# Block transposes on VectorE in place of TensorE's, in the second mixture of experts of a two-block network

## The chip, the core and the metric

The kernel runs on one core of a Trainium2 chip. The metric is the device time of one execution in microseconds (us). Three runs of the kernel before gave 2225.45, 2225.75 and 2227.01 us, median 2225.75.

## What is computed

Two blocks over 256 tokens of 1024 features, all in float32. The first block has gated linear attention, dilated attention and a mixture of 32 experts. The second block has two layers of three mixers each, followed by a dense feed-forward layer (layer 0) or a mixture of 8 experts (layer 1), a gated embedding and at the end a norm. The change touches the mixture of 8 experts:

```python
def moe_swiglu(x, router_w, router_b, w1, w3, w2):
    logits = (x @ router_w + router_b).astype(jnp.float32)
    top_v, top_i = lax.top_k(logits, TOP_K)
    top_p = jax.nn.softmax(top_v, axis=-1)
    gate = jnp.sum(jax.nn.one_hot(top_i, N_EXPERTS_2, dtype=jnp.float32) * top_p[..., None], axis=-2)
    out = jnp.zeros_like(x)
    for e in range(N_EXPERTS_2):
        out = out + gate[..., e:e + 1] * swiglu(x, w1[e], w3[e], w2[e])
    return out
```

where `swiglu(x, w1, w3, w2)` is `(silu(x @ w1) * (x @ w3)) @ w2`, with 1024 features, 2816 hidden features and 2 experts a token.

## The kernel before

The phases run one after another: block 1, its mixture (`moe1`), then mixers, feed-forward and embedding of layer 0, mixers of layer 1, the second mixture (`moe2`, phase `ffn1`), the embedding of layer 1 and the last norm. All large weights come through one `Stream` in the order of their use, in tiles of 1 MB, issued from SyncE's queue (L262). The stream has a ring of 3 buffers, which the phase `ffn1` widens by 6, so a tile can be issued when TensorE is done with the tile 9 before it.

`moe2` takes the experts in two halves of four (`c` = 0, 1), with 96 slots for each expert. The 384 slots of a half are three row tiles of 128 (`r`). At first the tokens are gathered into `xg`. Then a half has eleven passes (`j`), each over 256 of the 2816 hidden features. A pass has three parts:

- `first_products` multiplies the gathered tokens by eight tiles of `w1` and `w3` (`k`), 12 matmuls a tile, each on 32 columns of TensorE with 512 columns of weights moving. The sums are in three PSUM banks, slots on partitions: 256 columns for `w1` and 256 for `w3` of every row tile.
- ScalarE takes the SiLU of the first 256 columns into a tile `ft` (L301), and VectorE multiplies by the second 256 (L1981). `ft` has four buffers, and a pass uses three.
- `post` (L1984 to L1989) brings these onto partitions by hidden feature, as the second product needs them. Six 128x128 transposes on TensorE (L231) fill two PSUM banks, one of which ScalarE copies into `hT` and the other VectorE. `post` is kept in the list `later`, and `flush` runs it after two tiles of the following pass (`k == 2`).

After the eleven passes come the down products: two halves of the output features (`d`), each of 22 tiles `w2` against the 22 slices `hT[:, k]`. The last `post` of a half is flushed after two of these tiles. `combine` puts the results back to the tokens and adds them to `x`. In pass 5 of the second half stands `overflow`, a loop over the experts that got more than their 96 tokens, run 0 times or once. Its flag is loaded by every engine (L970) and followed by a branch that joins the engines (L971).

The scheduler of the language places each engine's instructions in a queue of its own, by the order of the program and by what it expects of their times; the waits between engines are semaphores that it sets. All eight PSUM banks are one ring, given out in turn by `bank`.

Of the kernel before, what the change touches and what calls it, by code (L numbers as in the profile page):

```python
# [14 lines left out]
PSUM = bass.MemoryType.PSUM  # L15

D, S = 1024, 256
RING = 3
# [3 lines left out]
# buffers of 1 MB that each phase adds to the ring's RING  # L22
WIDE = {"b1": 0, "moe1": 9, "mix0": 0, "mix1": 0, "ffn0": 2, "ffn1": 6, "ple0": 4, "ple1": 4, "fin": 0}
# buffers for the parts of weights; tokens that an expert takes at first
SPLIT = 4
CAP1, CAP2 = 32, 96
# the phases that begin with a router: its weights and their number
ROUTED = {"moe1": ("wr", 36), "ffn1": ("wr2", 8)}
# of the norms before the phases that take x split, with the norm's factors applied to the products
GAIN = {"b1": "n1g", "mix0": "g_mix0", "mix1": "g_mix1", "ffn0": "g_ffn0", "ple0": "g_ple0", "ple1": "g_ple1"}  # L30
# the mixers: buffers of 2 KB a partition, steps beside each step of a dense product (at first and later), attention units at once
V2, RATE, RATE2, LANES = 15, 1, 4, 2
# the mixers' outputs in the order in which their product with w_out takes them
# [5 lines left out]
# ---------------------------------------------------------------- host: layouts and shape constants  # L39
def _consts():  # L40
    f = np.float32
# [7 lines left out]
    # GLA: sums of log decays from the middle of a token's chunk, and from the middle of the chunk before  # L49
# [25 lines left out]
    # RWKV: sums from the middle of the chunk (token 63), inclusive and exclusive  # L75
# [4 lines left out]
    # of the 64 x 64 blocks on the diagonal  # L80
# [33 lines left out]
def _kt(w, kc):  # L114
    """[kc*128, C] -> [128, kc*C]"""
    c = w.shape[1]
    return w.reshape(kc, 128, c).transpose(1, 0, 2).reshape(128, kc * c)


def prep(I):  # L120
# [7 lines left out]
    # vectors, a column per 128 features  # L128
# [22 lines left out]
    # block 1: tiles in the order of their use; attention by heads  # L151
# [13 lines left out]
    # block 2  # L165
# [50 lines left out]
# ---------------------------------------------------------------- the program  # L216
class Bank:
    """One PSUM bank. The first matmul on a quadrant clears the bank's written bits there."""
# [15 lines left out]
class Stream:  # L234
    """The large weights in the order of their use, in tiles of up to 1 MB, through a ring of buffers that a
    phase can widen"""
# [39 lines left out]
class Kern:  # L276
# [6 lines left out]
    # ---- helpers  # L283
# [3 lines left out]
    def act(self, out, in_, func, **kw):  # L287
        """an activation; Ln and Exp from the table set that has both, loaded after the last of another set"""
# [16 lines left out]
    def after(self, ins):  # L305
        """what is traced inside goes behind ins in its engine's queue"""
        if ins is None or ins[0] is not self.nc.cur_bb:
            return ExitStack()
        return self.tc.issue_after(ins[1].ins if hasattr(ins[1], "ins") else ins[1])
# [13 lines left out]
    def rstd(self, src, n, scale, eps, floor=None, out=None):  # L323
        """1 / sqrt(src * scale + eps), src in PSUM, from an estimate and a Newton step"""
# [17 lines left out]
    def changed(self, x, k, n=2, late=False):  # L342
        """chunks k .. k + n - 1 of x are final: their squares for the next norm, and x * gain in two parts.
        late: the squares some steps of the next dense product later"""
# [29 lines left out]
    def add_squares(self):  # L374
# [4 lines left out]
        for i in range(sq.shape[1]):  # L379
# [4 lines left out]
            for t in range(2):  # L384
                ts = slice(128 * t, 128 * t + 128)
                b.mm(b.t[:, t:t + 1], sq[:, i, ts], ones[:, 0:1])
                # and their part of the router's logits
                self.lastsum = b.mm(b.t[:, 2 + n * t:2 + n * t + n], x[:, k + i, ts],
                                    self.sm1[:, o + n * (k + i):o + n * (k + i) + n])

    def sum_squares(self):
        """of x's features: for all partitions a row over the tokens, or, before a router, a column for each 128 of
        them, followed by the logits of x"""
# [9 lines left out]
    def factors(self, pool, more=None):  # L403
        """the norm's factor of each token, as rows and as columns, once the next dense product has begun"""
# [15 lines left out]
    def scaled(self, out, p):  # L420
        """products of the norm's input [128, n, 256], times the factors"""
        self.nc.vector.tensor_tensor(out, p, self.row[:, None, :].to_broadcast([128, p.shape[1], S]), op=ALU.mult)  # L422

    def weights(self, kc, ncol):
        """k, first column, then hi and lo parts of up to 512 columns of the k-th 128 rows of the next weights"""
# [14 lines left out]
    # ---- work that goes on beside the dense products: generators, advanced in turn between their steps  # L440
    def beside(self, gen, late=False):
        """late: the first part waits for its turn too"""
# [27 lines left out]
    def mm3(self, b, n, w, c, h, k):  # L470
        """chunk n of 128 features from a piece of weights that starts at column c, k-th chunk of the input"""
# [6 lines left out]
    def dense_fm(self, h, evict, kc=8, ncol=512, stagger=False):  # L478
        """features of the output on partitions; evict(n, ap) gets pairs of 128-feature chunks. stagger: the second
        half of the products goes pair by pair"""  # L480
# [17 lines left out]
    def dense_tm(self, h, evict, kc=8, ncol=512):  # L498
        """tokens on partitions; evict(t, ap[128, ncol]) per token tile"""
# [22 lines left out]
    # ---- the whole  # L522
# [100 lines left out]
    def prepare(self):  # L623
        """what later phases need of the small inputs"""
# [12 lines left out]
    # ---- block 1: gated linear attention, dilated attention, branch gates  # L637
    def block1(self, x, early):
        """early() makes room for the next phase's weights"""
# [66 lines left out]
    def gla(self, work, raw, h, a2, oraw, graw):  # L706
# [11 lines left out]
        def log_decay():  # L718
            """tokens on partitions"""
# [27 lines left out]
        def before(hd):  # L747
            """decays from and to the middles of the chunks"""
# [16 lines left out]
        def after(hd, kin, qin, qx, eB):  # L765
            hs = slice(hd * 128, hd * 128 + 128)
            # inside the chunks
# [11 lines left out]
            # between them: the state in the frame of the middle of each chunk  # L779
# [123 lines left out]
    # ---- the mixtures of experts  # L903
    def first_max(self, pool, x, n, tag):
        """max over the last axis of x [128, 2, n], and a one-hot of its first place"""
# [13 lines left out]
    def top2(self, pool, el, n):  # L919
        """the two largest of each token: one-hots and values"""  # L920
# [5 lines left out]
    def places(self, pool, oh1, oh2, n, beside):  # L926
        """each token's place in its experts' lists, from 1, and 0 where it is in none"""
# [17 lines left out]
    def shares(self, pool, oh1, oh2, m1, m2, n, group=None):  # L945
        """each token's weights of its two experts, by a softmax of their logits; times group"""
# [16 lines left out]
    def overflow(self, pool, x, xs, rs, wo, fi, n, units, w13, w2):  # L963
        """Experts with more than cap tokens: those past cap go through here, an expert at a time over all
        tokens, with weight 0 for the others. units loops over the fours of experts and, inside, over 256 hidden
        features of one of them at a time."""
# [55 lines left out]
    def route_in(self, work, x, n, b0, htm=None):  # L1022
        """RMS factors and logits with tokens on partitions; hi and lo of the tokens, not normed: the latter's last
        step is left to be done"""
# [26 lines left out]
    def gathered(self, out, htm, P, g):  # L1051
        """a one-hot's slots of tokens times g, feature-major: out's tiles [128, 8, n], each from a first slot, for
        P [128, 2, slots]"""
# [16 lines left out]
    def of_slots(self, out, P, col):  # L1070
        """a column of the tokens, gathered by a one-hot: for each 128 slots a column of out"""
# [7 lines left out]
    def keep_input(self, pool, x, g, rs):  # L1079
        """x * g, for the tokens past an expert's share"""  # L1080
# [5 lines left out]
    def over_flag(self, pool, Wt, ps, n, cap):  # L1086
        """weights of the tokens past their expert's first cap, and 1 if there are any"""
# [12 lines left out]
    def moe1(self, x):  # L1100
        tc, nc = self.tc, self.nc
        ident = self.cst("ident")
        with tc.tile_pool(reuse_waits="tile", name="m1", bufs=1) as pool:
# [4 lines left out]
            # only the chosen group's experts stay  # L1108
# [7 lines left out]
            # one-hots token -> (expert, slot), for 8 experts at first  # L1116
# [9 lines left out]
            def gather(n):  # L1126
                """the tokens of 8 experts"""
# [5 lines left out]
            def rest():  # L1133
# [4 lines left out]
                # a token's chosen group has the largest logit: its share is 1 / the sum of exp(logit - max)  # L1138
# [9 lines left out]
                # their weighted transposes  # L1148
# [88 lines left out]
    # ---- block 2: the three mixers  # L1237
    def rope(self):
        """the angles, to within pi, whose sines are cos and sin of position * frequency: [128 (2 heads x 64), 2, 256]"""
# [26 lines left out]
    def mix(self, l, x):  # L1266
        tc, nc, A = self.tc, self.nc, self.A
        with tc.tile_pool(reuse_waits="tile", name="mix", bufs=1) as pool:
# [17 lines left out]
            f = {}                              # tensors that are ready  # L1286
# [25 lines left out]
    def add_pairs(self, x, banks, late):  # L1312
        """the last products (pieces of weights, first column, input and its chunk) pair by pair, added to x"""
# [19 lines left out]
    def shifted(self, T, h):  # L1333
        """the RWKV columns, mixed with those of the token before"""
# [19 lines left out]
    def rwkv(self, T, z, w0, f, out):  # L1354
        """RWKV-7 in chunks of 128 tokens; heads 2c, 2c+1 are the halves of chunk c of the features"""
# [7 lines left out]
        # log decays (tokens on partitions), a and g  # L1363
# [17 lines left out]
        # normalised keys  # L1381
# [12 lines left out]
        # operands in the frame of the middle of each chunk, tokens (2, 128) last  # L1394
        dec = T("dec", (128, 2, 2, 2))         # feature chunk, token chunk: exp(end - mid), exp(mid - start)
        rT = self.cst("rT")
        tv = lambda ap: ap.rearrange("p (t s) -> p t s", t=2)
        ar, bk = [], []                        # token chunk, alpha | rho and beta | kappa
# [20 lines left out]
        # scores [j, i] of every head and chunk: beta.alpha, beta.rho, kappa.alpha, kappa.rho  # L1419
        sc = T("sc", (128, 8, 4, 128))         # token chunk and head  # L1420
# [13 lines left out]
        # inverse of I + L by doubling blocks up to 64, M and its transpose, for all heads and chunks  # L1434
# [18 lines left out]
        # beside it: tokens on partitions for v of both chunks, beta and kappa of the first; g; the bonus  # L1453
# [32 lines left out]
        # the two chunks in turn  # L1486
        yT = V2t("yT")
        st = T("st", (128, 2, 128))            # the state, heads on the diagonal blocks
        nc.gpsimd.memset(st, 0.0)
        for t in range(2):  # L1490
# [12 lines left out]
            # U0 = M0 R0, U1 = M1 (R1 - L10 U0)  # L1503
# [15 lines left out]
            if not t:  # L1519
                # the state after the first chunk, in the frame of the middle of the second  # L1520
# [12 lines left out]
            # y [v, i]  # L1533
# [525 lines left out]
```

## Time and profile before

| | |
|---|---|
| median of three runs | 2225.75 us |
| span of the profiled execution, first to last instruction | 2222.0 us |
| TensorE busy (matmuls) | 2066.5 us, 93% |
| VectorE busy | 825.3 us, 37% |
| ScalarE busy | 641.0 us, 29% |
| GpSimd busy | 23.7 us, 1% |
| moved by DMA | 613.39 MB, mean 276 GB/s |
| mean granted TensorE clock | 0.979 |

The time of the profiled execution itself is not listed apart from its span; the median of the runs is 3.75 us above the span. Busy shares are means over phases with different limits, so a change in one phase is read from that phase. Tile `w` is a weight tile, `ps` a PSUM bank, `xg`, `rawh` and `rawl` hold gathered tokens, `ft` the gated hidden features, `hT` their transposes. L228 is the matmul of the helper class `Bank` and L231 its transpose, L301 the helper for activations, so groups are told apart by their tiles.

### The profile page before, as it was taken

What the parts mean: (1) busy time and instruction counts of PE and PEld (TensorE: products, weight loads), DVE (VectorE), ACT (ScalarE), POOL (GpSimd) and SP (SyncE); (2) the same over time, 40 slices, a digit from 0 to 9 for tenths busy, and PEclk for the clock granted to TensorE, in tenths of its full rate; (3) what the DMA queues carried; (4) which work ended last, traced back from release to release, by engine and by line L of the source; (5) the groups of instructions that cost most, each with busy time, mean ns of one, the idle gap of its engine ahead of it and who ended that gap; (6) DMA issues with size and microseconds to landing.
All of it is one profiled execution on the core that took longest, in us unless ns stands there. A gap on an engine that the chain in (4) does not pass through costs nothing. (4 is left out here: it accounts for less than half of the span.)

```text
span 2222.0 us, 39268 instructions
## 1 busy us (share of the span) xinstructions
PE 2066.5 (93%) x16772; PEld 1250.0 (56%) x16772; DVE 825.3 (37%) x1736; ACT 641.0 (29%) x1320; POOL 23.7 (1%) x33
## 2 busy tenths in 40 slices
PE   7999998787577779999999999999999999999997
PEld 6999994122222238889999898743333333233236
DVE  5787663000000027777666877510000010000005
ACT  5466642000000025356556635310010000001005
POOL 0000000000000010000000000000000000000000
PEclk9999999999799999999999999899999999999999
DMA  5344577999899983325554331579999999799972
GB/s 175 117 143 152 185 308 298 420 420 419 357 420 419 420 348 114 107 67 205 193 184 171 130 117 58 207 280 382 392 400 383 388 369 384 294 419 393 406 307 93
DMA packets 88632, 613.39 MB, mean 276 GB/s; under 512 B 9879, under 2 KB 12071, under 8 KB 18560
## 3 DMA queue, kind: packets, MB, share of 16 engines
q1 hardware_dynamic: 86272, 604.74, 70.2%
q0 software_dynamic: 1344, 5.10, 0.7%
q8 instruction: 134, 2.20, 0.4%
q10 hardware_dynamic: 832, 0.94, 0.1%
q14 instruction: 50, 0.41, 0.1%
HBM read 609.69 MB, written 1.05 MB: 275 GB/s over the span
## 5 line engine op out<-in xcount | busy, mean ns | idle before, releaser
L228 PE MATMUL ps<-w,xg 128*32 128x512 f32 x2432 | 392.0, 599 | 67.5 <-DMA w<-wgu 43.0
L340 DVE TENSOR_TENSOR wl<-w,wh 128x512 fp32r<-128x512 f32 (+2 forms) x500 | 318.7, 652 | 166.5 <-ACT wh L339 158.0
L339 ACT CAST wh<-w 128x512 fp32r<-128x512 f32 (+2 forms) x500 | 289.7, 585 | 294.8 <-PE ps L228 229.4
L228 PE MATMUL ps<-w,hT 128*32 128x512 f32 x2624 | 338.5, 594 | 30.4 <-DMA w<-wdn 24.9
L228 PEld LDWEIGHTS ps<-w,xg 128*32 128x32 f32 x2432 | 89.2, 110 | 315.1 <-issue 199.0
L228 PE MATMUL ps<-rawh,wh 128*128 128x256 f32 x896 | 258.2, 288 | 0.0
L228 PE MATMUL ps<-rawh,wl 128*128 128x256 f32 x896 | 252.2, 282 | 1.5 <-DVE rawl L353 1.4
L228 PE MATMUL ps<-rawl,wh 128*128 128x256 f32 x896 | 252.1, 282 | 0.0
L228 PEld LDWEIGHTS ps<-w,hT 128*32 128x32 f32 x2624 | 90.4, 110 | 262.7 <-issue 188.5
L228 PE MATMUL ps<-w,rawl 128*32 128x512 f32 x1408 | 175.8, 599 | 5.4 <-issue 5.4
L228 PEld LDWEIGHTS ps<-rawh,wh 128*128 128x128 f32 x896 | 169.9, 190 | 4.2 <-issue 1.4
L228 PEld LDWEIGHTS ps<-rawh,wl 128*128 128x128 f32 x896 | 170.1, 190 | 3.2 <-DVE rawl L353 1.6
L228 PEld LDWEIGHTS ps<-rawl,wh 128*128 128x128 f32 x896 | 170.2, 190 | 1.1 <-DVE ast L1789 0.2
L228 PE MATMUL ps<-w,rawh 128*32 128x512 f32 x1408 | 168.3, 595 | 0.0
L1981 DVE SCALAR_TENSOR_TENSOR ft<-ps,rsl,ft 128x256 f32<-128x256 f32 x66 | 31.9, 484 | 313.6 <-ACT ft L301 313.2
L301 ACT ACTIVATE ft<-ps,rsl 128x256 f32<-128x256 f32 x66 | 31.3, 474 | 343.6 <-PE ps L228 343.6
L228 PE MATMUL ps<-hh,wh 128*128 128x256 f32 x416 | 125.8, 303 | 0.0
L228 PE MATMUL ps<-hh,wl 128*128 128x256 f32 x416 | 117.4, 284 | 0.1
L228 PE MATMUL ps<-hl,wh 128*128 128x256 f32 x416 | 117.2, 282 | 0.0
L228 PEld LDWEIGHTS ps<-w,rawl 128*32 128x32 f32 x1408 | 45.5, 110 | 103.6 <-issue 103.3
L228 PEld LDWEIGHTS ps<-w,rawh 128*32 128x32 f32 x1408 | 43.9, 110 | 97.9 <-issue 97.5
L1204 DVE SCALAR_TENSOR_TENSOR sg<-ps,rsl,sg 128x512 f32<-128x512 f32 x8 | 6.0, 750 | 206.7 <-PE ps L228 173.4
(495 smaller groups left out, 2727.0 us busy)
## 6 DMA issues: line engine op xcount, KB each, us to landing
w<-m SPq DMA_DIRECT2D x264, 1024.0 KB, 7.3
w<-wgu SPq DMA_DIRECT2D x128, 1024.0 KB, 19.9
w<-wdn SPq DMA_DIRECT2D x64, 1024.0 KB, 19.9
w<-f SPq DMA_DIRECT2D x32, 1024.0 KB, 5.2
w<-wz SPq DMA_DIRECT2D x20, 1024.0 KB, 4.9
w<-wdh SPq DMA_DIRECT2D x24, 768.0 KB, 4.3
w<-wb SPq DMA_DIRECT2D x16, 1024.0 KB, 4.9
w<-wo SPq DMA_DIRECT2D x8, 1024.0 KB, 5.3
```

Of the source, the lines that this page charges most:

```text
L228: return self.k.nc.tensor.matmul(out, lhsT, rhs, start=new, stop=stop, skip_group_check=True, **kw)
L301: r = sc.activation(out, in_, func, **kw)
L339: self.nc.scalar.copy(h, src)
L340: self.nc.vector.tensor_sub(l, src, h.bitcast(F32))
L1204: nc.vector.scalar_tensor_tensor(sg, acc[1].t, rsl[:, g:g + 1], sg, op0=ALU.mult, op1=ALU.mult)
L1981: nc.vector.scalar_tensor_tensor(t, g[r].t[:, 256:], u, t, op0=ALU.mult, op1=ALU.mult)
```

## The change

`post` no longer uses TensorE, PSUM or ScalarE. VectorE transposes `ft` into `hT` in blocks of 32 by 32, each written to the place that it has in the whole transpose. One instruction takes 32 slots by two blocks of 32 features (one in each half of the 256): 3 x 4 x 4 = 48 instructions a pass. The diff also drops comments and leaves blank lines for them, which changes nothing else.

```diff
                         def post(j=j, ts=ts):
-                            for i in range(2):
-                                b = self.bank()
-                                for r in range(3):
-                                    b.tr(b.t[:, 128 * r:128 * r + 128], ts[r][:, 128 * i:128 * i + 128], ident)
-                                (nc.vector.tensor_copy if i else nc.scalar.copy)(hT[:, 2 * j + i], b.t[:, :R])
+
+                            for r in range(3):
+                                for s in range(0, 128, 32):
+                                    for f in range(0, 128, 32):
+                                        nc.vector.transpose(hT[f:f + 32, 2 * j:2 * j + 2, 128 * r + s:128 * r + s + 32],
+                                                            ts[r].rearrange("p (i d) -> p i d", i=2)[s:s + 32, :, f:f + 32])
```

TensorE's queue from the third tile of pass 1 in the first half to the tile after it (`c_81` holds the identity), before:

```order
L228 MATMUL ps<-w,rawh 32x512 [waits DMAHW4_49]
L228 MATMUL ps<-w,rawh 32x512 x7
L228 MATMUL ps<-w,xg_13939 32x512 x4
L231 MATMUL ps<-c_81,ft 128x128 [waits DVE_49] x3
L231 MATMUL ps<-c_81,ft 128x128 [waits Activation_49]
L231 MATMUL ps<-c_81,ft 128x128 x2
L228 MATMUL ps<-w,rawh 32x512 [waits DMAHW5_49]
L228 MATMUL ps<-w,rawh 32x512 x7
```

and of the change:

```order
L228 MATMUL ps<-w,rawh 32x512 [waits DMAHW4_49]
L228 MATMUL ps<-w,rawh 32x512 x7
L228 MATMUL ps<-w,xg_13939 32x512 x4
L228 MATMUL ps<-w,rawh 32x512 [waits DMAHW5_49]
L228 MATMUL ps<-w,rawh 32x512 x7
L228 MATMUL ps<-w,xg_13939 32x512 x4
```

The six transposes between two tiles are gone, and the tiles follow one another in the order of before.

VectorE's queue around the branch in pass 5 of the second half, before:

```order
L1981 SCALAR_TENSOR_TENSOR ft<-ps,rsl,ft 128x256 [waits Activation_49] x3
L970 TENSOR_LOAD fi [waits DVE_49]
L971 COMPARE_AND_BRANCH
```

and of the change:

```order
L1981 SCALAR_TENSOR_TENSOR ft<-ps,rsl,ft 128x256 [waits Activation_49]
L1989 STREAM_TRANSPOSE hT<-ft 32x2x32 [waits DVE_49]
L1989 STREAM_TRANSPOSE hT<-ft 32x2x32 x2
L1981 SCALAR_TENSOR_TENSOR ft<-ps,rsl,ft 128x256 [waits Activation_49]
L1989 STREAM_TRANSPOSE hT<-ft 32x2x32 x4
L1981 SCALAR_TENSOR_TENSOR ft<-ps,rsl,ft 128x256 [waits Activation_49]
L1989 STREAM_TRANSPOSE hT<-ft 32x2x32
L970 TENSOR_LOAD fi [waits DVE_49]
L971 COMPARE_AND_BRANCH
```

Of the 48 block transposes of this pass 3 + 4 + 1 now stand ahead of the load of the flag, and 40 behind the branch. In the other passes all 48 stand behind the first gating and ahead of the next pass's.

TensorE's queue at the tiles 18 to 20 of the first down products, of the change:

```order
L228 MATMUL ps<-w,hT 32x512 [waits DMAHW4_49,DVE_49]
L228 MATMUL ps<-w,hT 32x512 [waits DVE_49] x11
L228 MATMUL ps<-w,hT 32x512 [waits DMAHW5_49]
L228 MATMUL ps<-w,hT 32x512 x11
L228 MATMUL ps<-w,hT 32x512 [waits DMAHW6_49,DVE_49]
L228 MATMUL ps<-w,hT 32x512 [waits DVE_49] x11
```

Here TensorE now waits for the block transposes of the passes 9 and 10, where it waited for copies of ScalarE and VectorE.

## Rows read from the trace of the kernel before

**Rows 1.** Stretches: start:end us, length, busy us (instructions) by engine, clock, DMA share, GB/s

```profile
1550.00:1600.00 50.00, 50.00 (x464) 15.63 (x460) 5.48 (x11) 5.22 (x11) 0.00 (x0) 1.00 1.00 399
...
1940.00:1945.00 5.00, 5.00 (x32) 1.15 (x28) 0.00 (x0) 0.00 (x0) 0.00 (x0) 0.61 0.98 401
1950.00:1980.00 30.00, 30.00 (x278) 9.12 (x274) 2.01 (x4) 1.90 (x4) 0.00 (x0) 1.00 1.01 418
1980.00:2010.00 30.00, 30.00 (x277) 9.16 (x270) 3.46 (x7) 3.32 (x7) 0.00 (x0) 1.00 1.01 418
2060.00:2110.00 50.00, 50.00 (x472) 15.21 (x468) 1.97 (x3) 2.06 (x3) 0.00 (x0) 1.00 1.01 408
```

**Rows 2.** TensorE's waits, 1460 to 2065 us: total us, times, longest

```profile
PE ps L228 <- issue: 5.4, 1, 5.4
```

**Rows 3.** Page: a group of the first mixture, and DMA issues (us to landing)

```profile
L228 PE MATMUL ps<-w,xg 128*32 128x512 f32 x2432 | 392.0, 599 | 67.5 <-DMA w<-wgu 43.0
...
w<-m SPq DMA_DIRECT2D x264, 1024.0 KB, 7.3
w<-wgu SPq DMA_DIRECT2D x128, 1024.0 KB, 19.9
```

**Rows 4.** TensorE's timeline, passes 1 and 2, first half: start us, us, instructions

```profile
1472.24 1.92 PE L228 MATMUL ps<-w,rawh 128*32 128x512 f32 x16
...
1474.84 1.90 PE L228 MATMUL ps<-w,rawh 128*32 128x512 f32 x16
...
1490.29 1.90 PE L228 MATMUL ps<-w,rawh 128*32 128x512 f32 x16
...
1492.98 0.87 PE L231 MATMUL ps<-c,ft 128*128 128x128 f32 x6
1493.78 1.92 PE L228 MATMUL ps<-w,rawh 128*32 128x512 f32 x16
```

**Rows 5.** TensorE's timeline, a pass of the second half with divided transposes

```profile
1893.17 0.66 PE L231 MATMUL ps<-c,ft 128*128 128x128 f32 x4
...
1896.47 0.44 PE L231 MATMUL ps<-c,ft 128*128 128x128 f32 x2
...
1915.00 0.66 PE L231 MATMUL ps<-c,ft 128*128 128x128 f32 x4
```

**Rows 6.** Groups by form, 1460 to 2065 us: busy us, mean ns, idle before

```profile
L231 PE MATMUL ps<-c,ft 128*128 128x128 f32 x132 | 21.9, 287 | 0.0
...
L1989 DVE COPY hT<-ps 128x384 f32<-128x384 f32 x22 | 12.3, 557 | 119.7 <-PE ps L231 119.7
L1989 ACT COPY hT<-ps 128x384 f32<-128x384 f32 x22 | 10.5, 478 | 88.2 <-PE ps L231 75.4 <-DMA w<-m 12.8
```

**Rows 7.** Small operations of VectorE (groups by form), and two of the timeline

```profile
L1097 DVE TENSOR_SCALAR fi<-ps 1x1 int32<-1x1 f32 x1 | 0.1, 147 | 0.0
...
L1700 DVE COPY cx<-sm 128x32 f32<-128x32 f32 x4 | 0.7, 178 | 0.1
L1726 DVE COPY vc<-ps 128x64 f32<-128x64 f32 x2 | 0.5, 226 | 0.2
L1532 DVE TENSOR_SCALAR st<-ps,dd 64x64 f32<-64x64 f32 x8 | 2.3, 283 | 0.1
...
1418.46 2.49 POOL L1046 TENSOR_TENSOR html<-mt,htmh 128x512 fp32r<-128x512 f32 x2 [71.09 <-DVE t2o L914]
1418.59 1.17 DVE L916 TENSOR_TENSOR t2o<-t2o,t2n 128x16 f32<-128x16 f32 x1
```

**Rows 8.** The branch of pass 5, second half: timelines, and SyncE's wait

```profile
1933.18 0.48 DVE L1981 SCALAR_TENSOR_TENSOR ft<-ps,rsl,ft 128x256 f32<-128x256 f32 x1 [13.85 <-ACT ft L301]
1934.04 0.48 DVE L1981 SCALAR_TENSOR_TENSOR ft<-ps,rsl,ft 128x256 f32<-128x256 f32 x1 [0.38 <-ACT ft L301]
1934.90 0.48 DVE L1981 SCALAR_TENSOR_TENSOR ft<-ps,rsl,ft 128x256 f32<-128x256 f32 x1 [0.38 <-ACTq L971]
...
1939.73 3.64 PE L228 MATMUL ps<-w,rawl 128*32 128x512 f32 x16 [5.41 <-issue]
...
SPq L971 <- DVEq L970: 6.7, 1, 6.7
```

## Prediction, made before the change was run

> **What bounds the kernel now.** I read the stretches first, then TensorE's waits and timeline, then the transfers, last VectorE's prices. The second mixture takes the end of the program. In its stretches TensorE is busy in every microsecond at a granted clock of 1.00, while VectorE works 2.0 to 5.5 us of 30 to 50 [rows 1], and between 1460 and 2065 us TensorE waits once, 5.4 us at the branch of the overflow loop [rows 2]. The reader should not stop there, since the 16 transfer engines are also counted 0.98 to 1.01 busy. Which of the two ends last is told by the transfers. A tile of this stage lands 7.3 us after its issue; in the first mixture, where TensorE does wait for weights (43.0 us), a tile needs 19.9 us [rows 3]. So here a transfer waits for TensorE to free one of 9 buffers, and TensorE is the bound: what leaves its queue leaves the time.
>
> **What is removed.** A tile of 1 MB is 12 matmuls of 512 columns. From 1474.84 to 1490.29 us six tiles pass, across the end of a pass, in 15.45 us: 2.575 us each, so 20.60 us for the 8 tiles of a pass [rows 4]. The real pass runs from 1472.24 to 1493.78, 21.54 us. The difference, 0.94 us, is the group of six transposes: 0.87 us of busy time, of which the next matmul overlaps a little, and a little more for changing over on either side. In other passes the scheduler splits the group 4 and 2 with one tile between. There a pass runs from 1893.17 to 1915.00, 21.83 us, and the transposes cost 1.23 us, because the change is paid twice [rows 5]. The timeline shows 10 undivided groups (nine at the start of the first half, one right after the branch) and 12 divided ones. So 10 x 0.94 + 12 x 1.23 = 9.4 + 14.8 = **24.2 us**. The grouped view shows 21.9 us busy for the 132 transposes [rows 6], which agrees: the rest is the change-over. The 22 copies on VectorE (12.3 us) and 22 on ScalarE (10.5 us) go too [rows 6]. They lie beside the matmuls and are worth nothing.
>
> A rule speaks against the edit. The Trainium skill, "VectorE: DVE Perf Modes", section "Rules for kernel authors", says to give a 128x128 transpose to TensorE if PSUM may be its destination; by it this kernel was right as it stood and the sum would be zero. Its section "The three transpose paths" gives 390 ns for one in bf16 on TensorE, by which the removed work would be an estimated 51 us. The trace has 24.2 us for it on the engine that never idles, and the sum goes by that.
>
> **What is added.** Per pass 48 block transposes on VectorE (3 row tiles x 4 x 4 blocks, 32 partitions x 2 x 32 elements), 1056 in all. No such operation is in the trace. Nearest rows: 147 ns for one element, 178 ns for a copy of 32 elements SBUF to SBUF, 226 ns for a copy of 64 from PSUM, 283 ns for 64x64 with a factor by partition [rows 7]. I take 180 ns, between the two plain copies and nearer the one that stays in SBUF; ends 147 and 283. A pass then costs VectorE 48 x 0.18 = 8.6 us (7.1 to 13.6) plus three gatings of 0.48 us, some 10 us beside 20.6 us of matmuls. What hides it is that length. The `ft` buffers are wanted again about a pass later (4 buffers, 3 a pass), and the down products reach the last two slices of `hT` only at their tiles 18 to 21, 18 x 2.575 = 46 us after they begin. If the cover were gone, each microsecond beyond 20.6 would be paid in every pass.
>
> The order of everything else stays. TensorE's tiles follow one another as before, without the transposes and their two PSUM banks a pass. The waits on ScalarE's copies become waits on VectorE's gating of two or three passes earlier, which is long done. SyncE's queue is the same, and so is where it stands at the branch.
>
> **The one place where the added work is on the path** is that branch (c = 1, pass 5). VectorE now has 8 block transposes ahead of its load of the flag (3 after the first gating, 4 after the second, 1 after the third), and SyncE was held 6.7 us until VectorE arrived there [rows 8]. Before, the gatings start at 1933.18, 1934.04 and 1934.90 and the last ends at 1935.38. With 0.18 us each the second starts at 1933.66 + 0.54 = 1934.20, the third at 1934.68 + 0.72 = 1935.40, and VectorE arrives at 1935.88 + 0.18 = 1936.06: **0.7 us later** (0.4 at 147 ns, 1.5 at 283 ns). If TensorE, which stands from 1934.3 to 1939.73, is released by something else, this is 0. I charge it in full. Queued behind VectorE's arrival are SyncE's next six tiles; TensorE found its next tiles waiting after the branch, and less than 1 us is no danger while a tile lands every 2.5 us at 418 GB/s [rows 1].
>
> After TensorE has stood for 5.4 us there, its granted clock averages 0.61 over 5 us [rows 1]: most of that stretch is at 1.2 GHz, the lower of its two levels, and sixteen matmuls take 3.64 us where others take 1.92 [rows 4, 8]. That costs 5 x 0.39 = 2.0 us. Whether the changed pause begins at a kinder or a worse moment I can't tell: 2 us less or 2 us more, in the range only.
>
> **Sum.** -24.2 + 0.7 = -23.5 us. The profiled execution spans 2222.0 us; the runs have a median of 2225.75, so 3.75 us lie around the span or between executions. Its span becomes 2198.5, the measured time 2225.75 - 23.5 = **2202.3 us**, 1.1% faster.
>
> **Rivals.** (1) The transfers become the bound. TensorE would ask for 1.0486 MB every 2.575 us, 407 GB/s. For it: all 16 engines look busy already at 399 GB/s [rows 1]. Were that the limit, a tile would take 2.628 us, a pass 21.02, and the gain would be 10 x 0.52 + 12 x 0.81 = 14.9 us: 2225.75 - 14.9 + 0.7 = 2211.6 us. Against it: after the branch they move 418 GB/s for 60 us, and the down products, which have no transposes, already run at 408 GB/s with TensorE never idle [rows 1]. I give it 6%. A page is sterner: the Trainium skill, "DMA: Bandwidth & Descriptors", section "Where 436 GB/s comes from", says that about 358 GB/s of HBM bind a transfer from HBM to SBUF. By that rule a pass could not be under 23.4 us, yet passes of 21.54 us run here; the trace disagrees with it, one core being alone on this chip.
>
> (2) Slower: VectorE becomes the bound. It decides when 48 t + 1.45 exceeds 20.60, that is at t = 0.40 us a block. Then ScalarE waits for `ft`, the gatings come late, and PSUM banks are not freed. For it: 48 small instructions where one was, of an unseen kind, and a VectorE operation of 16 elements that took 1.17 us while GpSimd worked beside it [rows 7]. At 0.45 us, twice the plain copy of 64, a pass is 48 x 0.45 + 1.45 = 23.05 us, and 22 x 2.45 - 24.2 = +29.7, 2255 us (less by what VectorE may lag). Against it: four rows of like size stand at 147 to 283 ns, and GpSimd has nothing to do in the passes. 4%.
>
> (3) The edit does nothing to the time, because a busy TensorE is not one at its peak and the transposes fill holes between matmuls. Then it is 2225.75 + 0.7 = 2226.5 us. Against it are the two pass lengths, 21.54 and 21.83 against 20.60 without transposes [rows 4, 5]. 4%.
>
> **Chances and range.** The forecast has 86%. Its own bounds are 2225.75 - 24.2 - 2.0 = 2199.6 (nothing at the branch, no slow spell) and 2225.75 - 24.2 + 1.5 + 2.0 = 2205.1; with some scatter of runs the range is 2198.5 to 2207. It leaves out the rivals, 14%, and little more. A measurement of this kernel can tell about 0.2%, 4.5 us, from no change. Forecast and rival 1 are faster: 0.92; rival 3 is the same: 0.04; rival 2 slower: 0.04.
>
> **What the profile after must show.** Passes of 20.6 us in both halves and no group of transposes on TensorE, else the first sum is wrong; TensorE still without waits but for the branch, and tiles landing in about 7 to 8 us, else rival 1 (19 us would prove it); block transposes under 0.28 us and VectorE done some 10 us into each pass, else rival 2; VectorE at the branch about 0.7 us later against TensorE's last matmul. A pass above 20.7 us, or a wait on VectorE inside the passes or at tile 18 of the down products, would make the prediction wrong.

## The result, and the profile after

The changed kernel takes 2200.8 us, median of four runs (2195.2 to 2205.2), against 2225.6 us for the kernel before (2223.8 to 2227.0). The ratio is 0.988, 95% interval 0.9862 to 0.9899 (the two medians alone give 0.989). The forecast was 2202.3 us, range 2198.5 to 2207.

The profiled execution took 2197.47 us, with a span of 2195.8 us. The first view to read is again the stretches of the second mixture (start:end us, length, busy us and instructions of PE, PEld, DVE, ACT and POOL, granted clock, DMA share, GB/s):

```profile
1550.00:1600.00 50.00, 50.00 (x472) 14.95 (x468) 33.85 (x138) 2.84 (x6) 0.00 (x0) 1.00 1.01 410
1925.00:1955.00 30.00, 30.00 (x284) 8.40 (x280) 15.99 (x66) 1.42 (x3) 0.00 (x0) 1.00 1.01 421
...
2040.00:2090.00 50.00, 50.00 (x461) 15.21 (x454) 2.63 (x4) 2.06 (x3) 0.00 (x0) 1.00 1.01 419
```

TensorE is busy throughout, as in [rows 1]. VectorE went from 5.48 to 33.85 us of 50, and the transfers from 399 to 410 GB/s, because the same tiles are asked for in less time. TensorE's waits in the stage after:

```profile
PE ps L228 <- issue: 5.6, 1, 5.6
```

It is still the one pause at the branch, 5.64 where it was 5.41 us [rows 2]. Transfers still wait for TensorE, not the reverse. In the page's list of DMA issues (KB each, median us from issue to landing) a tile lands 7.6 us after its issue, against 7.3 before [rows 3]:

```profile
w<-m SPq DMA_DIRECT2D x264, 1024.0 KB, 7.6
w<-wgu SPq DMA_DIRECT2D x128, 1024.0 KB, 19.9
```

TensorE's timeline of pass 1 in the first half (start us, us, instructions) answers to [rows 4]:

```profile
1463.89 1.90 PE L228 MATMUL ps<-w,rawh 128*32 128x512 f32 x16
...
1466.46 1.90 PE L228 MATMUL ps<-w,rawh 128*32 128x512 f32 x16
...
1484.49 1.90 PE L228 MATMUL ps<-w,rawh 128*32 128x512 f32 x16
```

Eight tiles take 1484.49 - 1463.89 = 20.60 us, as forecast, and between two tiles nothing is left. The new work by the grouped view (busy us, mean ns, idle before), and its place in VectorE's timeline of a pass:

```profile
L1989 DVE STREAM_TRANSPOSE hT<-ft 32x64 f32<-32x64 f32 x1056 | 249.1, 236 | 19.0 <-issue 2.0
```

```profile
1484.07 0.73 DVE L1989 STREAM_TRANSPOSE hT<-ft 32x64 f32<-32x64 f32 x3
...
1485.34 0.98 DVE L1989 STREAM_TRANSPOSE hT<-ft 32x64 f32<-32x64 f32 x4
...
1486.87 10.26 DVE L1989 STREAM_TRANSPOSE hT<-ft 32x64 f32<-32x64 f32 x41
1504.15 0.48 DVE L1981 SCALAR_TENSOR_TENSOR ft<-ps,rsl,ft 128x256 f32<-128x256 f32 x1 [7.01 <-ACT ft L301]
```

A block transpose takes 236 ns, and one starts every 0.25 us (41 in 10.26). So 48 fill 12 us of the pass, and VectorE then idles 7 us until the next pass's SiLU.

**A ruler for the stage.** Executions enter the second mixture at different times although nothing ahead of it is changed, so I measure the stage from the start of its first gating to the start of its last matmul on `hT`. Both stand in the tile view (op, count, ns min/median/max, first to last start). Of before:

```profile
L1981 DVE SCALAR_TENSOR_TENSOR ft<-ps,rsl,ft x66: 482/484/486, 1465.2 to 2051.4; 128x256 f32<-128x256 f32 x66
...
L228 PE MATMUL ps<-w,hT x2112: 592/592/617, 1681.9 to 2171.9; 128*32 128x512 f32 x192
```

and of after:

```profile
L1981 DVE SCALAR_TENSOR_TENSOR ft<-ps,rsl,ft x66: 483/484/486, 1462.9 to 2027.5; 128x256 f32<-128x256 f32 x66
...
L228 PE MATMUL ps<-w,hT x2112: 592/592/617, 1669.9 to 2145.6; 128*32 128x512 f32 x192
```

Before, the stage takes 2171.9 - 1465.2 = 706.7 us, after 682.7: 24.0 less. The first ten passes (to the first matmul on `hT`) go from 216.7 to 207.0 us, the rest from 490.0 to 475.7. The span shrank by 26.2 us. The other 2.3 are the earlier entry (1462.9 against 1465.2), and they are not the change's: the first gating of the first mixture, far ahead of the changed code, already starts at 364.2 where it was 366.5.

### The profile page after: what moved, and what is told of

Same layout as the page of the kernel before. It is cut to its first block, busy times and chain, and to the rows that moved or that the text cites. A ratio compares the mean times of both kernels' runs of the same rounds, so it can differ in the third digit from the quotient of the medians.

```text
span 2195.8 us, 40017 instructions
## 1 busy us (share of the span) xinstructions
PE 2040.8 (93%) x16640; PEld 1232.8 (56%) x16640; DVE 1061.7 (48%) x2770; ACT 630.8 (29%) x1298; POOL 23.8 (1%) x33
## 5 line engine op out<-in xcount | busy, mean ns | idle before, releaser
L228 PE MATMUL ps<-w,xg 128*32 128x512 f32 x2432 | 424.1, 600 | 67.8 <-DMA w<-wgu 43.1
L228 PEld LDWEIGHTS ps<-w,xg 128*32 128x32 f32 x2432 | 96.2, 110 | 316.6 <-issue 200.0
L1989 DVE STREAM_TRANSPOSE hT<-ft 32x64 f32<-32x64 f32 x1056 | 249.1, 236 | 19.0 <-issue 2.0
L228 PE MATMUL ps<-w,rawl 128*32 128x512 f32 x1408 | 201.3, 597 | 5.6 <-issue 5.6
L228 PEld LDWEIGHTS ps<-w,rawl 128*32 128x32 f32 x1408 | 54.0, 111 | 113.5 <-issue 112.0
```

Of the source, the lines that this page charges most:

```text
L228: return self.k.nc.tensor.matmul(out, lhsT, rhs, start=new, stop=stop, skip_group_check=True, **kw)
L1989: nc.vector.transpose(hT[f:f + 32, 2 * j:2 * j + 2, 128 * r + s:128 * r + s + 32], ts[r].rearrange("p (i d) -> p i d", i=2)[s:s + 32, :, f ...
```

## The experiments

The theory was that TensorE's queue alone sets the time of this stage, and VectorE's work lies beside it. The rivals were that the block transposes cost something themselves, that the gain is made elsewhere, and that the transfers already bound the stage.

| kernel | median us | ratio to before, 95% | first ten passes | rest | stage us |
|---|---|---|---|---|---|
| before | 2225.4 to 2227.3 | 1 | 216.7 | 490.0 | 706.7 |
| changed, again | 2203.9 | 0.9892 (0.9874 to 0.9909) | 206.9 | 474.8 | 681.7 |
| no transposes | 2201.2 | 0.9872 (0.9853 to 0.989) | 206.9 | 475.1 | 682.0 |
| both kinds | 2226.0 | 0.9992 (0.9979 to 1.0005) | 216.6 | 489.4 | 706.0 |
| first half only | 2215.2 | 0.9937 (0.9919 to 0.9956) | 206.9 | 488.8 | 695.7 |
| 72 blocks | 2200.5 | 0.9879 (0.9858 to 0.99) | 206.9 | 475.7 | 682.6 |
| 96 blocks | 2259.2 | 1.0144 (1.0122 to 1.0165) | 230.3 | 506.7 | 737.0 |
| first mixture too | 2202.5 | 0.9885 (0.9864 to 0.9906) | 206.9 | 475.4 | 682.3 |
| eleven of twelve | 2206.0 | 0.9899 (0.9877 to 0.992) | 206.1 | 479.3 | 685.4 |
| eight of twelve | 2156.0 | 0.9695 (0.9666 to 0.9724) | 191.1 | 449.0 | 640.1 |

The kernel before ran beside each set: 2227.3 us for the first four, 2226.7 for the next four, 2225.4 for the last. The three right columns are read from one profiled execution each, as above.

### The changed kernel again

No edit.

> The changed kernel once more, with more rounds, for the size of the gain and for the spread of its runs, which was 10.0 us in four where the kernel before spread 3.3 us. Theory (TensorE is the bound and lost 24.2 us of transposes): 24 us under the kernel before, 2201 us, with passes of 20.60 us. Rival (the transfers are now close to a bound, and the spread comes from executions in which they fall behind): the times form two groups some 8 us apart, and the median can lie anywhere from 2196 to 2205.

It took 2203.9 us where the kernel before took 2227.3, 23.4 less. Five of its six runs lie between 2200.4 and 2204.7 and one at 2209.3, so they don't form two groups some 8 us apart. The 17 of the kernel before spread more, 2222.4 to 2234.9, so the spread needs no change. In neither profiled execution of the changed kernel does TensorE wait for a weight in the stage, and the profiled execution of the run with the first mixture changed too, which took 2210.1 us, has a stage of 682.3 us like the others. The rival falls. What differs is the entry: in the profiled executions of the kernel before, of the changed one and of the table's rows down to 96 blocks, which are alike up to the stage, the first gating starts anywhere from 1462.9 to 1471.8 us, while the stage behind it repeats within 1 us where TensorE's work is the same. Of these 8.9 us 3.4 are there at the first gating of the first mixture (364.2 against 367.6), and 5.5 come later. In the router ahead of the stage the granted clock differs. In the execution without transposes, which enters at 1471.8:

```profile
1410.00:1420.00 10.00, 10.00 (x53) 10.00 (x51) 2.61 (x6) 1.26 (x2) 0.00 (x0) 0.53 1.00 419
1420.00:1430.00 10.00, 7.37 (x34) 6.91 (x34) 5.43 (x28) 3.79 (x9) 2.50 (x2) 0.50 0.24 98
1430.00:1440.00 10.00, 9.78 (x59) 6.14 (x62) 3.72 (x16) 1.46 (x4) 0.00 (x0) 0.78 0.17 52
```

and in the first of the changed kernel, which enters at 1462.9:

```profile
1410.00:1420.00 10.00, 6.42 (x45) 5.96 (x44) 6.67 (x27) 3.84 (x10) 2.49 (x2) 0.81 0.64 266
1420.00:1430.00 10.00, 9.45 (x48) 6.00 (x52) 3.37 (x15) 1.47 (x4) 0.00 (x0) 0.68 0.08 11
1430.00:1440.00 10.00, 10.00 (x79) 5.93 (x72) 3.59 (x9) 1.47 (x4) 0.00 (x0) 1.00 0.63 214
```

The clock is the column before the last two. By these averages it was at its lower level (0.50 of full, 1.2 GHz) for an estimated 24 of the 30 us in the one, and in the other for 10 and for 3 more from 1400 to 1410 us. Some 10 us more at half the clock would be worth 5 us. It isn't the whole of the spread: the second look at the changed kernel enters at 1466.9 us with no more of the lower clock there than the first.

### No transposes, and both kinds at once

```diff
 def post(j=j, ts=ts):
-    for r in range(3):
-        ...
+    pass
```

> Leaves out the transposes altogether: post does nothing, and hT is filled with zeros once, so the down products multiply zeros. Theory (all of VectorE's block transposes lie beside matmuls): the same time as the changed kernel, 2201 us, within 1 us; at the branch VectorE comes 1.3 us earlier than with the change, of which TensorE's pause of 5.64 us shows 0.2. Rival (48 small instructions a pass do cost something, by memory that they share with TensorE's operands or by lateness): up to 5 us less than the changed kernel, 2196 us.

```diff
 def post(j=j, ts=ts):
+    for i in range(2):
+        b = self.bank()
+        for r in range(3):
+            b.tr(b.t[:, 128 * r:128 * r + 128], ts[r][:, 128 * i:128 * i + 128], ident)
+        (nc.vector.tensor_copy if i else nc.scalar.copy)(hT[:, 2 * j + i], b.t[:, :R])
     for r in range(3):
         for s in range(0, 128, 32):
             for f in range(0, 128, 32):
-                nc.vector.transpose(hT[...], ...)
+                nc.vector.transpose(junk[...], ...)
```

> TensorE transposes and the copies are made as before, and beside them VectorE makes the 48 block transposes a pass into a spare tile that nobody reads. Theory (what counts is TensorE's queue): the time of the kernel before, 2226 us, within 2 us; passes of 21.54 or 21.83 us, VectorE some 14 us busy in each. Rival (the block transposes cost time where they run): 2231 us or more, as much above the kernel before as leaving them out takes off the changed kernel.

Without any transposes the stage takes 682.0 us, with them on VectorE 682.7 and 681.7. The median is 2.7 us lower than the changed kernel's, but the intervals of the two ratios overlap, and the stage does not show it. With both kinds the stage has its old length, 706.0 us, and the passes have their six transposes on TensorE again, while VectorE makes all its blocks beside them. The grouped view of that kernel:

```profile
L1994 DVE STREAM_TRANSPOSE junk<-ft 32x64 f32<-32x64 f32 x1056 | 249.3, 236 | 25.2 <-issue 2.0
...
L231 PE MATMUL ps<-c,ft 128*128 128x128 f32 x132 | 21.9, 287 | 0.0
```

249 us of new work on VectorE cost nothing, and 21.9 us on TensorE cost all of the 24. The theory stands, and the rival of dear block transposes falls.

### The first half only

```diff
-def post(j=j, ts=ts):
+def post(j=j, ts=ts, c=c):
+    if c:
+        for i in range(2):
+            ...
+        return
     for r in range(3):
```

> The change is made in the first half (c = 0) alone; the second half keeps TensorE's transposes and the copies. Theory (each group of transposes costs 0.94 us undivided, 1.23 us divided, where it stands): the first half held nine undivided and two divided groups, 9 x 0.94 + 2 x 1.23 = 10.9 us, so 2225.6 - 10.9 = 2214.7 us; passes of 20.60 us in the first half, of 21.54 or 21.83 us in the second. Rival (the gain is made somewhere else, at the branch or in the weights' lead after it): all of it or none, 2201 or 2225 us.

2215.2 us; the stage lost 706.7 - 695.7 = 11.0 us where 10.9 was expected. The first ten passes, with nine undivided groups and one divided one, lost 9.8 us (9 x 0.94 + 1.23 = 9.7), and the rest lost 1.2: the one divided group that the first half leaves to its down products. So the gain stands where the groups stood, and 0.94 and 1.23 us are right one by one.

### How much room VectorE has

72 block transposes a pass, the additional 24 into a spare tile:

```diff
+    for r in (0, 1):
+        for s in range(0, 128, 32)[:3]:
+            for f in range(0, 128, 32):
+                nc.vector.transpose(junk[f:f + 32, :, 128 * r + s:128 * r + s + 32], ...)
```

> The changed kernel with half as many block transposes again: 24 more a pass, of the same ft into a spare tile. Theory (VectorE is free up to the length of a pass): at the measured spacing of 0.25 us a pass costs VectorE 72 x 0.25 + 1.45 = 19.5 us, under the 20.6 us of the matmuls, so the time stays where the changed kernel is, 2203.9 us on this chip, and VectorE idles 1 us a pass. Rival (the waits between gating, transposes and SiLU add up before VectorE is full, since ft has four buffers for three a pass): each pass grows by the missing part, some 0.5 us or more, 2215 us.

and 96, the additional 48 likewise:

```diff
+    for r in range(3):
+        for s in range(0, 128, 32):
+            for f in range(0, 128, 32):
+                nc.vector.transpose(junk[...], ...)
```

> The changed kernel with twice the block transposes: 48 more a pass, into a spare tile. Theory (VectorE becomes the bound where 48 t + 1.45 is over 20.60): a pass costs VectorE 96 x 0.25 + 1.45 = 25.5 us, 4.9 more than the matmuls. VectorE may fall behind by about one pass, 20 us, before TensorE lacks a PSUM bank, so in the first half four passes are free and six cost 4.9 each, 29 us; in the second half the branch of pass 5 makes TensorE wait for what VectorE is behind, some 25 us, and the passes behind it are free again. Together about 54 us, 2258 us (2312 if VectorE may not fall behind at all: 22 x 4.9 = 108). TensorE's waits then name VectorE, and the pause at the branch is over 20 us. Rival (VectorE has room that its busy time hides): 2204 us.

With 72 the stage is unchanged, 682.6 us, and VectorE's idle time ahead of a pass is down to 1.0 us. Its timeline there:

```profile
1506.46 0.48 DVE L1982 SCALAR_TENSOR_TENSOR ft<-ps,rsl,ft 128x256 f32<-128x256 f32 x1 [1.04 <-ACT ft L301]
```

With 96 the kernel is slower than before, 2259.2 us where 2258 was expected. TensorE's timeline there, first half:

```profile
1600.16 1.94 PE L228 MATMUL ps<-w,xg 128*32 128x512 f32 x8 [5.23 <-DVE ft L1982]
1626.28 1.64 PE L228 MATMUL ps<-w,xg 128*32 128x512 f32 x8 [2.36 <-DVE ft L1982]
1652.40 1.06 PE L228 MATMUL ps<-w,xg 128*32 128x512 f32 x8 [3.61 <-DVE ft L1982]
1678.51 1.94 PE L228 MATMUL ps<-w,xg 128*32 128x512 f32 x8 [5.31 <-DVE ft L1982]
```

The waits begin only at 1600 us, some six passes after the stage began at 1468.5, and from then on a pass lasts 1626.28 - 1600.16 = 26.12 us. So VectorE may fall behind by about one pass, and what it needs is a little more than the 25.5 us that I summed. TensorE's waits in the stage:

```profile
PE ps L228 <- DVEq L971: 30.4, 1, 30.4
PE ps L228 <- DVE ft L1982: 20.5, 5, 5.3
```

There are five waits, not six: four in the passes and the fifth in the first tile of the down products. They come to 20.5 us, and behind most of them the granted clock is low (0.50 from 1600 to 1605 us), which fills the rest of VectorE's longer pass. From its first gating TensorE needs 481.2 us to the branch where it needed 452.0, 29 more, and there it stands 30.4 us, 25 more than in the changed kernel, both as expected. So the prediction's second rival, VectorE as the bound, is real; it starts between 72 and 96 blocks.

### What the branch waits for

The prediction charged VectorE's later arrival in full. Five executions tell. VectorE's timeline in the changed kernel, and behind it TensorE's:

```profile
1917.03 0.24 DVE L1989 STREAM_TRANSPOSE hT<-ft 32x64 f32<-32x64 f32 x1
1919.29 10.01 DVE L1989 STREAM_TRANSPOSE hT<-ft 32x64 f32<-32x64 f32 x40 [2.03 <-issue]
```

```profile
1920.56 3.64 PE L228 MATMUL ps<-w,rawl 128*32 128x512 f32 x16 [5.64 <-issue]
```

VectorE's last work ahead of the flag ends at 1917.27, and TensorE goes on 3.29 us later. Before, it was 1935.38 and 4.35 us [rows 8]. Without transposes, where VectorE arrives as early as before, the pause is 5.17 us, in the second look at the changed kernel 5.18. With 96 blocks, VectorE and TensorE:

```profile
1979.37 0.24 DVE L1989 STREAM_TRANSPOSE hT<-ft 32x64 f32<-32x64 f32 x1
```

```profile
1980.13 3.64 PE L228 MATMUL ps<-w,rawl 128*32 128x512 f32 x16 [30.43 <-DVEq L971]
```

There TensorE goes on 0.52 us after VectorE's last work. So TensorE can follow VectorE within some 0.5 us, and where VectorE is early it stands 5.2 to 5.6 us for another reason, which the profile calls issue. (With both kinds, 5.44 us, it names VectorE's block transposes; but the last of them ahead of the flag had ended 3.1 us before TensorE went on.) VectorE had some 2.8 us to spare in the changed kernel (3.29 - 0.5). What that other reason is was not tried.

### The same edit where the transfers are the bound

```diff
-b = self.bank()
 hT = work.tile([128, 4, 128], F32, name="hT", tag="hT")
-for k in range(4):
-    b.tr(b.t[:, k * 128:k * 128 + 128], sg[:, k * 128:k * 128 + 128], ident)
-self.cp(hT, b.t.rearrange("p (k c) -> p k c", k=4))
+for i in (0, 2):
+    for s in range(0, 128, 32):
+        for v in range(0, 128, 32):
+            nc.vector.transpose(hT[v:v + 32, i:i + 2, s:s + 32],
+                                sg.rearrange("p (k d) -> p k d", k=4)[s:s + 32, i:i + 2, v:v + 32])
```

> The changed kernel, with the same edit in the first mixture as well: 32 block transposes in each of its eight groups in place of four transposes on TensorE and a copy on ScalarE. There TensorE waits for weights, 43.1 + 24.6 us, and it waits for hT at once. Theory (the bound decides, and there it is the transfers): TensorE stands some 8 - 1.5 = 6.5 us longer in each group, which the ring of 12 tiles takes up, since TensorE needs 1.84 us for a tile that takes 2.49 us to come; nothing is gained, and at most the last group's delay is paid, 0 to 3 us, 2204 to 2207 us. Rival A (transposes off TensorE are worth their time wherever they stand): 8 x 0.66 = 5 us less, 2199 us. Rival B (the chain through hT is on the path): 8 x 6.5 = 52 us more, 2256 us.

2202.5 us, as the changed kernel within its spread. TensorE's waits in the first mixture of this kernel:

```profile
PE ps L228 <- DMA w<-wgu: 41.5, 70, 1.6
...
PE ps L228 <- DMA w<-wdn: 19.4, 32, 1.3
PE ps L228 <- DVE hT L1209: 16.6, 8, 3.1
```

TensorE now waits for block transposes, 2.1 us a group and not the 6.5 I had worked out, since the first tiles need the first blocks only. The waits for weights are shorter in turn. Rival A's 5 us can't be told from the times, but from the first mixture's own length, first to last gating (tile view), in the changed kernel and in this one:

```profile
L1204 DVE SCALAR_TENSOR_TENSOR sg<-ps,rsl,sg x8: 742/751/752, 364.2 to 790.8; 128x512 f32<-128x512 f32 x8
```

```profile
L1204 DVE SCALAR_TENSOR_TENSOR sg<-ps,rsl,sg x8: 743/750/752, 367.0 to 794.0; 128x512 f32<-128x512 f32 x8
```

426.6 and 427.0 us. To the last matmul on `hT` of that mixture, which takes in the last group's delay, it is 447.4 and 447.9. So neither rival shows. The same edit that gives 24 us in one stage gives nothing in another.

### What comes next

```diff
-    tiles(g, [(hT[:, k], 0)], w)
+    tiles(g, [(hT[:, k], 0)], w, 11 if k else 12)
```

(likewise in `first_products`; the last argument is the number of matmuls)

> The changed kernel, in which the last of the twelve matmuls of a weight tile in the second mixture is left out in all tiles but the first of each sum, so the last 32 slots of a half are computed wrong. TensorE would need 11/12 x 2.575 = 2.36 us for a tile. Theory (after the change the transfers are next, at the 420 GB/s that they reach in the first mixture, 1.0486 MB in 2.497 us): 264 tiles x (2.575 - 2.497) = 20.6 us less at most, 2183 us, with TensorE waiting for w and tiles landing some 20 us after their issue. Rival (the transfers have more in hand): TensorE stays the bound and gains 154 x 0.215 + 84 x 0.215 = 51 us, 2153 us, with tiles landing in 8 us.

Neither came true: 2206.0 us, and a tile still takes 2.57 us, from 1504.31 to 1506.88. TensorE's timeline of one:

```profile
1504.31 2.27 PE L228 MATMUL ps<-w,rawh 128*32 128x512 f32 x15
1506.39 0.61 PE L228 MATMUL ps<-w,xg 128*32 128x512 f32 x3
...
1506.88 2.27 PE L228 MATMUL ps<-w,rawh 128*32 128x512 f32 x15
```

The premise was wrong. The trace has two records of 592 ns for each matmul of the program, 24 for a weight tile, yet the tile takes 2.575 us, so several run at a time: the records come in fours, on 32 columns each, every 0.43 us. Four matmuls of the program thus take 0.858 us, and four with one left out take as long. The Trainium skill, "TensorEngine Tiling (Array Packing)", section "Key Properties", says that such tiles of TensorE work independently and in parallel. The trace agrees: three take the time of four. The kernel's stage is 2.7 us longer than the changed kernel's; in this execution TensorE stood a second time behind the branch, 2.24 us. Then with a whole row of four left out:

```diff
-    tiles(g, [(hT[:, k], 0)], w)
+    tiles(g, [(hT[:, k], 0)], w, 8 if k else 12)
```

> The changed kernel, in which the four matmuls of the third row tile are left out in all weight tiles of the second mixture but the first of each sum, so the last 128 slots of a half are computed wrong. The run with eleven of twelve showed that four matmuls on 32 columns each take 0.858 us beside one another, and three as long as four; eight take 2 x 0.858 = 1.72 us a tile in place of 2.575. Theory (TensorE is the bound after the change, and the transfers, at 2.497 us for 1.0486 MB as in the first mixture, are the next one close behind): TensorE waits for w, tiles land some 20 us after their issue, the stage saves 264 x (2.575 - 2.497) = 20.6 us, some 7 us more by the nine tiles that are there at its start, and up to 7 us because the pause at the branch no longer counts: 2169 to 2183 us. Rival A (2.575 us a tile is what the transfers take already): no change, 2204 us. Rival B (the transfers have much in hand in this stage): 264 x 0.858 x 0.95 = 215 us less, 1990 us.

2156.0 us. TensorE's waits in the stage, and the landing of its tiles:

```profile
PE ps L228 <- DMA w<-m: 107.1, 184, 1.5
PE ps L228 <- SPq L971: 16.6, 1, 16.6
```

```profile
w<-m SPq DMA_DIRECT2D x264, 1024.0 KB, 17.9
```

Both rivals fall: the stage does get faster, so 2.575 us was TensorE's, and by 42.6 us and not 215, because now it waits for weights and tiles land after 17.9 us. The mechanism was right, the size short. Over the stage the transfers move 411 GB/s. They run at 418 to 420 nearly throughout; at the branch, where TensorE stands for 16.6 us, they fall to 273 GB/s from 1890 to 1900 us and to 180 from 1900 to 1910. So the transfers set nearly all of the stage's length, and the pause still costs something. The changed kernel's stage has 256 tiles at 2.575 us, 659.2 of its 682.7 us; the rest is the pause, the slow clock behind it and TensorE's other work, which combines the results. That work lies beside the transfers now; I had counted the pause, but not the work. How the 42.6 us divide was not tried. So some 42 us is what there is to gain from TensorE before the transfers set the stage's time.

## Why the prediction was right

The mechanism held: TensorE sets the stage's time, and VectorE's work lies beside it. That the median came within 1.5 us of the forecast is in part luck, since runs of this kernel differ by 10 us; the stage's own length is what bears out the sum.

- **TensorE is the bound of the stage.** Right. It was read from the landing times, and the waits after, the run with both kinds and the run with eight of twelve show it.
- **Removed: 24.2 us.** Right: the stage lost 24.0 and 25.0 us in two executions, and the first half alone 11.0 of an expected 10.9. The copies that went with the transposes were not tried apart; TensorE's groups account for the whole gain and leave nothing for them.
- **The rule against the edit.** By the rule of the Trainium skill, "VectorE: DVE Perf Modes", section "Rules for kernel authors", that a 128x128 transpose belongs on TensorE, the sum would have been zero; the measured 24 us decide against it here, because TensorE is the engine that never idles.
- **Added: 48 blocks of 180 ns.** The size was off: 236 ns, and 0.25 us from one to the next, so 12 us a pass and not 8.6. It lay within the ends (147 and 283). A block instruction handles 64 elements a partition, and the row with as many, the copy of 64 at 226 ns, came nearest; I leaned on the copy of 32. It cost nothing, because the cover of 20.6 us held, and the run with 72 shows that it would have held at half as much again.
- **The branch: 0.7 us, charged in full.** This step failed, by little. Behind TensorE's last matmul VectorE arrived 1.3 us later than before (2.35 against 1.06), more than forecast, yet the pause was 5.64 and 5.18 us against 5.41. The prediction named the other possibility (released by something else, then 0), and that is what the runs show: VectorE has 2.8 us to spare. So this term was 0, and what does release TensorE stays open. The slow clock behind the branch came as before: sixteen matmuls took 3.64 us again.
- **Rival 1, the transfers.** Not here: 410 to 421 GB/s without a wait. It is what comes next, some 42 us away.
- **Rival 2, VectorE the bound.** Not at 48 blocks, but real: with 96 the kernel takes 2259 us. Its price was too high, though. It charged all 22 passes, by which 96 blocks would give 2312 us, and named what VectorE may lag only in brackets. The run shows about a pass of it. So blocks of 0.45 us would have cost less than the 2255 forecast; that it lies near the 2259 is chance.
- **Rival 3, nothing.** The transposes filled no holes: a pass fell to 20.60 us.

## What to carry to other kernels

Ask of each stage which engine or transfer ends last, and price an edit by that alone: 249 us of work put on an engine with time to spare cost nothing, 21.9 us taken off the one without gave 24, and the same edit in a stage that waits for weights gave nothing. The room of the engine that takes the work is the length of the loop's pass, plus about one pass of lag where buffers allow it, up to the next point that joins the engines. Where a forecast rests on a stage, measure the stage between two of its own instructions; the whole time had several times the scatter.

## What the runs showed that I had not expected

- Leaving out one of four matmuls on 32 columns saves nothing: they take 0.858 us, with three or four of them.
- A block transpose of 32 x 64 float32 elements takes 236 ns with 0.25 us from one to the next, alone or while TensorE transposes the same tile.
- The entry to the stage moves by up to 9 us between executions that are alike until then, in part along with the granted clock in the router. The runs of one kernel differ by as much.
